# Query scores of the expert router issued one unit later in PSUM banks of their own, and two small reads of the attention at highest priority

## The chip, the cores and the metric

The kernel runs on one core of one Trainium2 chip. The metric is the device time of one execution in microseconds, shown as the median of the runs. The core has a matrix engine (TensorE, PE in the profile, with its weight loads on a row of their own, PEld), a vector engine (VectorE, DVE), an activation engine (ScalarE, ACT), GpSimd (POOL) and a queue for transfers (SyncE, SP). Each engine takes its own instructions strictly in the order in which they stand in its queue. TensorE writes to PSUM, eight banks of 128 partitions by 512 words of fp32.

## The reference

Two transformer blocks over 512 tokens of width 1024, batch 1. The first has a mixer of retention and sparse attention and a convolutional feed-forward part. The second has a mixer and then PEER, a layer that picks 16 of 16384 experts for each of 8 heads. The two places that the change touches are these, cut to what matters:

```
# first block, sparse attention, for a block of 128 queries
p_cmp = masked_softmax(q @ kc^T, valid_c)        # 31 compressed keys
p_slc = masked_softmax(q @ ks^T, mask)           # selected keys
p_win = masked_softmax(q @ kw^T, mask)           # window
...
# second block, PEER router
q = (x @ w_query).reshape(T, 8, 2, 128)
s = einsum('thpk,hpnk->thpn', q, sub_keys)       # 16 score groups of 128 keys
top_s, top_i = top_k(s, 16)
cand = top_s[:, :, 0, :, None] + top_s[:, :, 1, None, :]
best_s, best_pos = top_k(cand, 16)
gate = softmax(best_s)
```

## The kernel before

All matrix products with large weights are made of three passes: a weight tile of 128 by 1024 words (a unit) is loaded into `raw` (L192), ScalarE rounds it to `whi` (L200), VectorE or GpSimd takes the rest `wlo = raw - whi` (L201), and TensorE multiplies low by high, high by low and high by high (L206 to L208). `raw` has three buffers, `whi` and `wlo` eight each, so units are split up to eight ahead of their use. `proj_t` is one unit against all its tokens: 24 matmuls.

The instructions are written as a program in Python, and a planner then makes the order of each engine's queue: it simulates the engines and gives each free engine the ready instruction that stands earliest in the program. So an instruction can overtake earlier ones that are not ready in the simulated time. `high_priority` puts the instructions under it ahead of all others that are ready. What the planner believed of the durations fixes the order; the chip then follows that order with its own durations.

**Attention** (`attend`, tiles `tt` = 3, 2, 1, 0 of 128 queries). For a tile, four matmuls give the compressed scores (L599) into a bank of the group `as_` (banks 0, 1, 3 in turn). VectorE adds the mask bias in two instructions (L601). Then for each of two key groups, two branches and four heads: scores of 128 by 512 (L633, L635) into the next bank of the same group, the negated row maximum on VectorE (L637, `nm`), the exponential on ScalarE (L639), transposes (L647) and the product with the values (L654). The third head's scores of the first tile take bank 0 again, which the compressed scores held. The last tiles of retention (`retain`) stand just before: their normalisation is on VectorE (L575 to L584), with a power on GpSimd in the middle (L579).

**Router** (`route`). Sixteen units of the query weights: a projection of 24 matmuls into a bank of group `t` (banks 6, 7 in turn), a copy to `q` by ScalarE (L1100), four score matmuls (8 records of L1103) into the other bank of `t`, a copy to `sc` (L1105), and for each of four token tiles a top 16 on VectorE, five operations in `top16` (L1174 to L1178). After the sixteen units come the candidate sums, second top 16 and index arithmetic of four token tiles, nearly all on VectorE (L1111 to L1155); each `si` (L1141) is transposed by TensorE (L1166). Then `gates_dense` builds the dense gates from one-hot tiles (matmuls L1216, on tiles made by VectorE, ScalarE and GpSimd), spills them to memory, and `experts_out` reads them back and runs the output side of the experts.

`peer` puts 64 units of the experts' input side (`expert_in`, 24 matmuls of 384 columns, activation L1062) between the steps of `route` and `gates_dense`. The list `pace` says how many in how many steps: 3 in the first step, 2 in the next 15, 45 in the 32 after, 14 in the 24 steps of `gates_dense`. These last 14 use tiles of a pool that is opened when `route` has ended.

Of the kernel before, what the change touches and what calls it, by code (L numbers as in the profile page):

```python
# [2 lines left out]

# [4 lines left out]
F32 = mybir.dt.float32  # L8
# [4 lines left out]
AF = mybir.ActivationFunctionType  # L13
ALU = mybir.AluOpType
AX = mybir.AxisListType
# [3 lines left out]
S = 512  # L19
D = 1024  # L20
NT = 4
# [150 lines left out]
class Block:  # L172
# [413 lines left out]
    def attend(self, T, psp):  # L586
        tc, nc, a = self.tc, self.nc, self.a
# [3 lines left out]
        for tt in range(NT - 1, -1, -1):  # L591
            tok = slice(128 * tt, 128 * tt + 128)
            nk = 128 * (tt + 1)
            sums = T.tile([128, 3, 8], F32, name="sums")

            s = T.tile([128, 8, 32], F32, name="cs")
            ps = psp.tile([128, 4, 2, 32], F32, name="as_")
            for i in range(4):
                nc.tensor.matmul(ps[:, i], self.nqT[:, i, tok], self.kcT, start=True, stop=True)  # L599
            for g in range(2):  # L600
                nc.vector.tensor_tensor(s[:, 4 * g:4 * g + 4, :], ps[:, :, g, :],  # L601
                                        self.cst["cbias"][:, None, 32 * tt:32 * tt + 32].to_broadcast([128, 4, 32]),
                                        op=ALU.add)
            m = T.tile([128, 8], F32, name="cm")
            nc.vector.tensor_reduce(m, s, AX.X, ALU.max)
            nc.vector.tensor_tensor(s, s, m[:, :, None].to_broadcast([128, 8, 32]), op=ALU.subtract)
# [2 lines left out]
                                    op=ALU.mult)  # L609
# [15 lines left out]
            for g in range(2):  # L625
                pos = psp.tile([128, 2, 4, 64], F32, name="ao")
                for br in range(2):
                    po = pos[:, br]
                    for i in range(4):
                        h = 4 * g + i  # L630
                        ps = psp.tile([128, 512], F32, name="as_")
                        for part in range(2):
                            nc.tensor.matmul(ps[:, :nk], self.hl[:, h, tok], self.hh[:, 4 * part + 2 * g + br, :nk],  # L633
                                             start=part == 0, stop=False)
                        nc.tensor.matmul(ps[:, nk - 128:nk], self.identb, self.maskb, start=False, stop=True)  # L635
                        nm = T.tile([128, 1], F32, name="nm", bufs=4)
                        nc.vector.tensor_reduce(nm, ps[:, :nk], AX.X, ALU.max, negate=True)  # L637
                        p = T.tile([128, 512], F32, name="p", bufs=4)
                        e = nc.scalar.activation(p[:, :nk], ps[:, :nk], AF.Exp, bias=nm,  # L639
                                                 accum_out=sums[:, 1 + br, h:h + 1])  # L640
                        if tt == NT - 1 and g == 1:
                            k = 4 * br + i
                            with tc.issue_after(e.ins):
                                wout.append(self.unit(a["w_out"][k], eng=nc.gpsimd if i in WP else None))
                        pt = psp.tile([128, 4, 128], F32, name="at")
                        for b in range(tt + 1):
                            nc.tensor.transpose(pt[:, b, :], p[:, 128 * b:128 * b + 128], self.ident)  # L647
                        pT = T.tile([128, 4, 128], F32, name="pT", bufs=3)
                        if h % 2:
                            nc.vector.tensor_copy(pT[:, :tt + 1], pt[:, :tt + 1])  # L650
                        else:
                            nc.scalar.activation(pT[:, :tt + 1], pt[:, :tt + 1], AF.Copy)
                        for b in range(tt + 1):
                            nc.tensor.matmul(po[:, i, :], pT[:, b, :], self.vv[:, b, 128 * br + 64 * g:128 * br + 64 * g + 64],  # L654
                                             start=b == 0, stop=b == tt)
                    hs = slice(4 * g, 4 * g + 4)
                    sm = sums[:, 1 + br, hs]
                    nc.vector.tensor_scalar(sm, sm, 1e-30, None, op0=ALU.max)
                    nc.vector.reciprocal(sm, sm)
                    nc.vector.tensor_tensor(sm, sm, gt[:, 1 + br, hs], op=ALU.mult)  # L660
                    t = T.tile([128, 4, 64], F32, name="yt")
                    nc.vector.tensor_tensor(t, po, sm[:, :, None].to_broadcast([128, 4, 64]),
                                            op=ALU.mult)
                    nc.gpsimd.tensor_tensor(y[:, hs], y[:, hs], t, op=ALU.add)
                if tt and g == 0:
                    self.queries(T, tt - 1)
# [355 lines left out]
    def peer(self):  # L1022
        tc, nc, a = self.tc, self.nc, self.a
        dt = slice(128, S)
        n = S - 128
        with ExitStack() as c0:
            dr = c0.enter_context(tc.tile_pool(name="pdr", bufs=1, space=DRAM))
            self.actD = dr.tile([NSPILL, 128, n], F32, name="actD")
            self.gD = dr.tile([12, 128, 4096], F32, name="gD")
            P = c0.enter_context(tc.tile_pool(name="pe", bufs=1, reuse_waits="tile"))  # L1030
            self.acc0 = P.tile([128, D], F32, name="acc0")
            self.eid = P.tile([128, 128], I32, name="eid")
            self.gate0 = P.tile([128, 128], F32, name="gate0")
            with ExitStack() as c1:
                Q = c1.enter_context(tc.tile_pool(name="pra", bufs=1, reuse_waits="tile"))
                psp = _Banks(self.psum, t=[6, 7], u=[4, 5, 0], g=[1, 2, 3])
                sel = [Q.tile([128, NT - 1, 128], F32, name=f"sel{i}") for i in range(3)]
                iota = self.const(Q, "iota")
                pace = [(1, 3), (15, 2), (32, 45), (24, 14)]
                self.pend = []  # L1040
                work = [self.route(Q, psp, sel, iota), self.gates_dense(psp, sel, iota)]
                j, self.gpool = 0, None
                for n_, (steps, us) in enumerate(pace):
                    for i in range(steps):
                        _advance(work)
                        for _ in range((i + 1) * us // steps - i * us // steps):
                            act = self.expert_in(self.gpool or Q, psp, 2 * j, nc.vector if n_ == 2 else nc.gpsimd,
                                                 "ga" if self.gpool else "act")
                            nc.sync.dma_start(self.actD[j], act)
                            j += 1  # L1050
                assert j == NSPILL
                while work:
                    _advance(work)
            self.experts_out()
# [33 lines left out]
    def route(self, Q, psp, sel, iota):  # L1088
        tc, nc, a = self.tc, self.nc, self.a
        with tc.tile_pool(name="rt", bufs=1, reuse_waits="tile") as R:  # L1090
            sk = R.tile([128, 16, 128], F32, name="sk")
            nc.sync.dma_start(sk, a["skT"].rearrange("p (m n) -> p m n", m=16))
            val = R.tile([128, NT, 16, 16], F32, name="val")
            idx = R.tile([128, NT, 16, 16], U32, name="idx")
            for m in range(16):
                w = self.unit(a["w_q"][m])
                ps = psp.tile([128, S], F32, name="t")
                self.proj_t(ps, w, self.hh, self.hl)
                q = R.tile([128, S], F32, name="q", bufs=2)
                nc.scalar.activation(q, ps, AF.Copy)  # L1100
                ps = psp.tile([128, NT, 128], F32, name="t")
                for t in range(NT):
                    nc.tensor.matmul(ps[:, t, :], q[:, 128 * t:128 * t + 128], sk[:, m, :], start=True, stop=True)  # L1103
                sc = R.tile([128, NT, 128], F32, name="sc", bufs=2)
                nc.scalar.activation(sc, ps, AF.Copy)  # L1105
                for t in range(NT):
                    self.top16(R, sc[:, t, :], val[:, t, m, :], idx[:, t, m, :])
                yield
            for t in range(NT):
                cand = R.tile([128, 8, 16, 16], F32, name="cand")  # L1110
# [17 lines left out]
                for i in range(2):  # L1128
                    eq = R.tile([128, 8, 16, 16], F32, name="eq")
                    for h in range(0, 8, 4):  # L1130
# [4 lines left out]
                                                op=ALU.is_equal)  # L1135
                    nc.vector.tensor_tensor(eq, eq, fi[:, i::2, None, :].to_broadcast([128, 8, 16, 16]),
                                            op=ALU.mult)
# [6 lines left out]
                g = Q.tile([128, 8, 16], F32, name="g", bufs=2)  # L1144
# [160 lines left out]
def _advance(work, n=1):  # L1305
    while n and work:
        try:
            next(work[0])
            n -= 1
        except StopIteration:  # L1310
            work.pop(0)
# [54 lines left out]
```

## Time and profile before

| | us |
|---|---|
| median of three runs | 2283.4 |
| lowest, highest | 2283.37, 2287.0 |
| profiled execution, its time | 2284.21 |
| its span, first to last instruction | 2282.4 |
| TensorE busy in the span | 2201.8 (96%) |
| VectorE busy | 1680.1 (74%) |
| ScalarE busy | 922.4 (40%) |
| GpSimd busy | 690.0 (30%) |
| mean granted TensorE clock | 0.986 |

Busy time of a matmul is from its start to its modelled end, and consecutive ones overlap; the spacing of their starts says how fast they follow each other. The time of an execution is 1.8 us more than its span.

### The profile page before, as it was taken

Reading aid. Unit: us, or ns where it says so; the run is one execution under the profiler, and the core shown is the slowest. Engines: PE = TensorE matmul, PEld = TensorE weight load, DVE = VectorE, ACT = ScalarE, POOL = GpSimd, SP = SyncE. Lnnn points to the kernel's source line nnn. Section 1 sums busy time; section 2 is a strip of 40 time slices with the busy share of each in tenths; the row PEclk is TensorE's granted clock in tenths of the full one; section 3 lists DMA queues with packets and bytes.
Section 4 is the critical chain, followed back from the end, with each engine's and each line's share of the span. In section 5 each row is a group of like instructions: output and inputs, shape, how many; then the busy total and the mean of one; then the engine's idle time right before and its main releaser. Section 6 shows DMA issues by size and latency. Waiting matters only on the chain. (4 is left out here: it accounts for less than half of the span.)

```text
span 2282.4 us, 32112 instructions
## 1 busy us (share of the span) xinstructions
PE 2201.8 (96%) x11849; PEld 1952.1 (86%) x11849; DVE 1680.1 (74%) x3126; ACT 922.4 (40%) x1540; POOL 690.0 (30%) x558
## 2 busy tenths in 40 slices
PE   7998999999999999989999989889999999999997
PEld 6786878888889888877999989878888888888886
DVE  5347557888426478567799999678888787888888
ACT  4225444333325443342344468533333333333332
POOL 2223110000002223210000587533444444444445
PEclk9998999999999999999999999989999999999999
DMA  8324006767322221042355546799999999999996
GB/s 274 99 69 120 10 1 210 246 210 230 102 92 87 92 84 56 10 159 85 128 171 180 161 174 252 290 325 349 338 340 343 355 333 339 330 345 335 346 340 216
DMA packets 165645, 469.53 MB, mean 206 GB/s; under 512 B 18800, under 2 KB 62704, under 8 KB 165360
## 3 DMA queue, kind: packets, MB, share of 16 engines
q1 hardware_dynamic: 128624, 333.25, 42.7%
q0 software_dynamic: 36864, 134.23, 16.0%
q8 instruction: 93, 1.52, 0.3%
q14 instruction: 64, 0.52, 0.1%
HBM read 422.31 MB, written 39.85 MB: 202 GB/s over the span
## 5 line engine op out<-in xcount | busy, mean ns | idle before, releaser
L206 PE MATMUL b<-hh,wlo 128*128 128x384 f32 (+2 forms) x1872 | 655.5, 351 | 6.3 <-DVE wlo L201 3.1
L207 PE MATMUL b<-hl,whi 128*128 128x384 f32 (+2 forms) x1872 | 652.9, 349 | 3.3 <-DVE hl L288 3.2
L208 PE MATMUL b<-hh,whi 128*128 128x384 f32 (+2 forms) x1872 | 652.3, 349 | 0.0
L201 DVE TENSOR_TENSOR wlo<-raw,whi 128x1024 fp32r<-128x1024 f32 x375 | 455.3, 1222 | 201.4 <-ACT whi L200 195.4
L200 ACT ACTIVATE whi<-raw 128x1024 fp32r<-128x1024 f32 (+1 forms) x405 | 425.3, 1054 | 363.2 <-PE b L208 148.9
L206 PEld LDWEIGHTS b<-hh,wlo 128*128 128x128 f32 x1872 | 353.4, 189 | 34.2 <-DVE wlo L201 3.7
L207 PEld LDWEIGHTS b<-hl,whi 128*128 128x128 f32 x1872 | 354.2, 189 | 30.4 <-DVE hl L288 3.8
L208 PEld LDWEIGHTS b<-hh,whi 128*128 128x128 f32 x1872 | 353.9, 189 | 24.7
L206 PE MATMUL b<-whi,wl 128*128 128x512 f32 x768 | 299.9, 390 | 12.3 <-DVE wl L1262 12.3
L208 PE MATMUL b<-whi,wh 128*128 128x512 f32 x768 | 300.9, 392 | 0.0
L207 PE MATMUL b<-wlo,wh 128*128 128x512 f32 x768 | 300.8, 392 | 0.0
L201 POOL TENSOR_TENSOR wlo<-raw,whi 128x1024 fp32r<-128x1024 f32 x30 | 80.0, 2678 | 640.7 <-ACT whi L200 635.7
L1074 POOL DMA_INDIRECT grow<-in_p_ur_dram,eid x128 | 177.2, 1385 | 234.7 <-DVE gact L1077 166.9
L1074 POOL DMA_INDIRECT grow<-in_p_v_dram,eid x128 | 172.1, 1345 | 217.8 <-DVE acc L1079 132.8
L1062 ACT ACTIVATE act<-b 128x384 f32<-128x384 f32 x114 | 55.7, 492 | 382.4 <-PE b L208 301.4
L206 PE MATMUL b<-whi,hl 128*128 128x512 f32 (+1 forms) x464 | 178.9, 387 | 3.3 <-DVE hl L254 2.3
L206 PEld LDWEIGHTS b<-whi,wl 128*128 128x128 f32 x768 | 144.9, 189 | 41.4 <-DVE wl L1262 12.6
L208 PE MATMUL b<-whi,hh 128*128 128x512 f32 (+1 forms) x464 | 177.9, 384 | 0.0
L207 PE MATMUL b<-wlo,hh 128*128 128x512 f32 (+1 forms) x464 | 177.7, 383 | 0.0
L208 PEld LDWEIGHTS b<-whi,wh 128*128 128x128 f32 x768 | 144.7, 188 | 30.4
L207 PEld LDWEIGHTS b<-wlo,wh 128*128 128x128 f32 x768 | 144.8, 189 | 29.0
L1079 DVE SCALAR_TENSOR_TENSOR acc<-grow,gact,acc 128x1024 f32<-128x1024 f32 x127 | 162.7, 1281 | 3.4 <-DMA grow<-in_p_v_dram,eid 2.4
(296 smaller groups left out, 2953.6 us busy)
## 6 DMA issues: line engine op xcount, KB each, us to landing
raw<-in_p_u_dram SPq DMA_DIRECT2D x128, 512.0 KB
raw<-in_p_v_dram SPq DMA_DIRECT2D x128, 512.0 KB
raw<-in_w_adaT_dram SPq DMA_DIRECT2D x48, 512.0 KB
gD<-gst SPq DMA_DIRECT2D x48, 512.0 KB
gt<-gD SPq DMA_DIRECT2D x16, 1536.0 KB
raw<-in_w_up_dram SPq DMA_DIRECT2D x44, 512.0 KB
raw<-in_w_t_dram SPq DMA_DIRECT2D x32, 512.0 KB
acts<-actD SPq DMA_DIRECT2D x64, 192.0 KB
```

Of the source, the lines that this page charges most:

```text
L200: nc.scalar.activation(hi, raw, AF.Copy)
L201: (eng or nc.vector).tensor_tensor(lo, raw, hi.bitcast(F32), op=ALU.subtract)
L206: mm(out, al, bh, start=start, stop=False)
L207: mm(out, ah, bl, start=False, stop=False)
L208: mm(out, ah, bh, start=False, stop=stop)
L1062: self.nc.scalar.activation(act, ps, AF.Gelu)
L1074: nc.gpsimd.indirect_dma_start(out=g, out_offset=None, in_=rows[n], in_offset=bass.IndirectOffsetOnAxis(ap=self.eid[:, s:s + 1], axis=0))
L1079: nc.vector.scalar_tensor_tensor(self.acc0, g, act[:, s:s + 1], self.acc0, op0=ALU.mult, op1=ALU.add)
```

## The change

In `attend`, for the first tile (`tt` = 3) alone, the two bias additions of the compressed scores and the first four row maxima are put under `high_priority`. In `route`, the loop has 17 steps in place of 16: step m projects unit m and then issues the scores and the top 16 of unit m - 1; the scores are in banks of group `g` (1, 2, 3), which `gates_dense` uses later, and no longer in those of `t`. `pace` has 16 steps in place of 15 for the two experts' units, since `route` now has one step more.

```
+            with tc.high_priority() if tt == NT - 1 else nullcontext():
+                for g in range(2):
+                    nc.vector.tensor_tensor(s[...], ps[:, :, g, :], cbias, op=ALU.add)
...
-                        nc.vector.tensor_reduce(nm, ps[:, :nk], AX.X, ALU.max, negate=True)
+                        with tc.high_priority() if tt == NT - 1 and g + br == 0 else nullcontext():
+                            nc.vector.tensor_reduce(nm, ps[:, :nk], AX.X, ALU.max, negate=True)
...
-                pace = [(1, 3), (15, 2), (32, 45), (24, 14)]
+                pace = [(1, 3), (16, 2), (32, 45), (24, 14)]
...
-            for m in range(16):
-                w = self.unit(a["w_q"][m])
-                ps = psp.tile([128, S], F32, name="t")
-                self.proj_t(ps, w, self.hh, self.hl)
-                q = R.tile([128, S], F32, name="q", bufs=2)
-                nc.scalar.activation(q, ps, AF.Copy)
-                ps = psp.tile([128, NT, 128], F32, name="t")
-                for t in range(NT):
-                    nc.tensor.matmul(ps[:, t, :], q[:, 128 * t:128 * t + 128], sk[:, m, :], start=True, stop=True)
-                sc = R.tile([128, NT, 128], F32, name="sc", bufs=2)
-                nc.scalar.activation(sc, ps, AF.Copy)
-                for t in range(NT):
-                    self.top16(R, sc[:, t, :], val[:, t, m, :], idx[:, t, m, :])
+            qs = {}
+            for m in range(17):
+                if m < 16:
+                    w = self.unit(a["w_q"][m])
+                    ps = psp.tile([128, S], F32, name="t")
+                    self.proj_t(ps, w, self.hh, self.hl)
+                    qs[m] = R.tile([128, S], F32, name="q", bufs=2)
+                    nc.scalar.activation(qs[m], ps, AF.Copy)
+                if m:
+                    q = qs.pop(m - 1)
+                    ps = psp.tile([128, NT, 128], F32, name="g")
+                    for t in range(NT):
+                        nc.tensor.matmul(ps[:, t, :], q[:, 128 * t:128 * t + 128], sk[:, m - 1, :], start=True, stop=True)
+                    sc = R.tile([128, NT, 128], F32, name="sc", bufs=2)
+                    nc.scalar.activation(sc, ps, AF.Copy)
+                    for t in range(NT):
+                        self.top16(R, sc[:, t, :], val[:, t, m - 1, :], idx[:, t, m - 1, :])
                 yield
```

## Rows read from the trace of the kernel before

**Rows 1.** The page, busy time of each engine.
```profile
PE 2201.8 (96%) x11849; PEld 1952.1 (86%) x11849; DVE 1680.1 (74%) x3126; ACT 922.4 (40%) x1540; POOL 690.0 (30%) x558
```
**Rows 2.** Windows: stretch, length, busy PE, PEld, DVE, ACT, POOL, PE clock, DMA share, GB/s.
```profile
1062.00:1137.00 75.00, 74.74 (x400) 67.93 (x401) 49.55 (x238) 24.75 (x36) 2.40 (x1) 1.00 0.33 107
1137.00:1313.00 176.00, 176.00 (x1017) 175.43 (x1015) 173.65 (x388) 75.22 (x110) 30.81 (x10) 1.00 0.52 171
1313.00:1322.00 9.00, 0.82 (x3) 0.52 (x3) 8.93 (x13) 2.33 (x4) 5.86 (x5) 0.62 0.21 67
1322.00:1462.00 140.00, 139.44 (x1069) 138.69 (x1069) 135.51 (x359) 107.49 (x232) 119.75 (x99) 0.99 0.61 234
1491.00:2260.00 769.00, 769.00 (x3704) 677.65 (x3705) 627.18 (x814) 270.17 (x373) 343.39 (x251) 1.00 0.93 337
```
**Rows 3.** Waits of PE, 994 to 1330 us: total us, times, longest.
```profile
PE b L1166 <- DVE si L1141: 6.1, 1, 6.1
PE b L1103 <- ACT q L1100: 5.7, 8, 0.7
```
**Rows 4.** Timeline of PE, score matmuls: start, us, what, idle before.
```profile
1025.44 1.16 PE L1103 MATMUL b<-sk,q 128*128 128x128 f32 x8 [0.58 <-ACT q L1100]
...
1054.90 1.16 PE L1103 MATMUL b<-sk,q 128*128 128x128 f32 x8 [0.75 <-ACT q L1100]
...
1072.72 1.05 PE L1103 MATMUL b<-sk,q 128*128 128x128 f32 x8
...
1135.04 1.05 PE L1103 MATMUL b<-sk,q 128*128 128x128 f32 x8
```
**Rows 5.** Timeline of ACT, activations of successive experts' units.
```profile
1149.88 0.49 ACT L1062 ACTIVATE act<-b 128x384 f32<-128x384 f32 x1 [2.72 <-issue]
...
1166.52 0.49 ACT L1062 ACTIVATE act<-b 128x384 f32<-128x384 f32 x1 [2.72 <-issue]
```
**Rows 6.** Timeline of DVE, first and last work for one unit.
```profile
1041.10 1.23 DVE L201 TENSOR_TENSOR wlo<-raw,whi 128x1024 fp32r<-128x1024 f32 x1 [1.45 <-ACT whi L200]
1042.25 0.87 DVE L1174 MAX8 val<-sc 128x8 f32<-128x128 f32 x4
...
1046.73 0.28 DVE L1178 FIND_INDEX8 idx<-val,rest 128x8 uint32<-128x128 f32 x1
```
**Rows 7.** Timeline of DVE, end of the router: one shape, twice.
```profile
1298.05 2.35 DVE L1134 TENSOR_TENSOR eq<-abf,c_iota 128x1024 f32<-128x1024 f32 x2
...
1307.36 6.82 DVE L1134 TENSOR_TENSOR eq<-abf,c_iota 128x1024 f32<-128x1024 f32 x2
```
**Rows 8.** Timeline of PE, end of the router and first gates.
```profile
1319.11 0.45 PE L1166 MATMUL b<-c_ident,si 128*128 128x128 f32 x1 [6.07 <-DVE si L1141]
1321.66 4.52 PE L1216 MATMUL b<-gb,ga 128*128 128x128 f32 x22 [2.11 <-DVE gb L1213]
...
1335.01 5.89 PE L1216 MATMUL b<-gb,ga 128*128 128x128 f32 x48
```
**Rows 9.** Timeline of PE, scores of the first attention tile.
```profile
188.29 1.19 PE L633 MATMUL b<-hh,hl 128*128 128x512 f32 x2 [4.99 <-DVE cs L601]
...
198.56 0.71 PE L633 MATMUL b<-hh,hl 128*128 128x512 f32 x2
```
**Rows 10.** Timeline of DVE at the same place.
```profile
185.53 1.36 DVE L582 TENSOR_SCALAR rraw<-b,bmv,gr 128x128 f32<-128x128 f32 x4 [1.55 <-POOL gr L579]
...
187.66 0.49 DVE L601 TENSOR_TENSOR cs<-b,c_cbias 128x128 f32<-128x128 f32 x2
188.06 1.28 DVE L637 TENSOR_REDUCE nm<-b 128x1 f32<-128x512 f32 x2
```
**Rows 11.** Timeline of ACT at the same place.
```profile
188.81 1.28 ACT L639 ACT_TABLE_LOAD   x1 [12.38 <-issue]
190.11 0.69 ACT L639 ACTIVATE p<-b,nm 128x512 f32<-128x512 f32 x1
```
**Rows 12.** Windows after the wait; columns as in rows 2.
```profile
188.30:196.00 7.70, 6.38 (x21) 4.08 (x22) 6.53 (x13) 5.28 (x12) 1.28 (x1) 0.52 0.19 43
```

More of the change, by code (lines that the diff above doesn't have):

```diff
@@ L1 @@
 import numpy as np
-from contextlib import ExitStack
+from contextlib import ExitStack, nullcontext
 import concourse.bass as bass
@@ L599, in attend @@
                 nc.tensor.matmul(ps[:, i], self.nqT[:, i, tok], self.kcT, start=True, stop=True)
[L600 to L603, printed above, removed]
+            with tc.high_priority() if tt == NT - 1 else nullcontext():
+                for g in range(2):
+                    nc.vector.tensor_tensor(s[:, 4 * g:4 * g + 4, :], ps[:, :, g, :],
+                                            self.cst["cbias"][:, None, 32 * tt:32 * tt + 32].to_broadcast([128, 4, 32]),
+                                            op=ALU.add)
             m = T.tile([128, 8], F32, name="cm")
```

## The prediction

> **What bounds the kernel now.** I read the page first: TensorE is busy 96% of the span and no other engine comes near [rows 1]. An average hides where the other 4% lie, so next come the windows, cut where the work changes. From 1491 to 2260 us TensorE has no gap, with the transfers at 0.93 of their engines; nothing in the change touches that stretch. In the router, TensorE is busy throughout from 1137 to 1313, and VectorE nearly so (173.65 of 176). Then TensorE stands still for most of nine microseconds while VectorE works on (0.82 against 8.93 of 9.00), and from 1322 to 1462 both are full again [rows 2]. So VectorE is late once, at 1313, and TensorE sets the pace around it. The view of waits names the places: eight waits of the score matmuls for `q`, and one long wait for the last `si` of the router [rows 3]. A second one of that size stands in the attention, 4.99 us before the third head's scores [rows 9]. These three places are what the change can reach.
>
> **The router's scores.** The change takes the wait for `q` from between projection and scores; the instructions are the same. The waits shown add to 5.7 us [rows 3], but the start-to-start spacing is the better measure, since a busy time includes the pipeline's end. Where the scores directly follow their projection, a unit takes (1054.90 - 1025.44) / 4 = 7.365 us; five starts are in that run. Where the planner has put one experts' unit in between, it takes (1135.04 - 1072.72) / 6 = 10.387 us [rows 4]. An experts' unit alone takes (1166.52 - 1149.88) / 4 = 4.16 us [rows 5]. So a unit without a gap costs 10.387 - 4.16 = 6.23 us, and the gap costs 7.365 - 6.23 = 1.14 us. Eight gaps [rows 3] are 9.1 us. The other eight units are already covered by experts' units and gain nothing. After the change the next projection is the cover; it needs a free bank of `t` and a `w` tile, and both are there, as `t` now serves projections alone and units are split eight ahead. For the last unit, the second experts' unit of the new `pace` entry can fill the gap. If that cover were missing, one gap of 1.14 us would stay.
>
> Is VectorE fast enough? Its work for one unit runs from 1041.10 to 1047.01, 5.91 us [rows 6], against 6.23 us of TensorE. It just fits, so the scores stage stays TensorE's.
>
> **The wait at 1313.** The saving above starts VectorE's long tail sooner, and by more than 9.1 us. Before, eight experts' units ran among the scores; their only reason was the gap. Without gaps I expect the two that the program puts there. The last scores, which end at 1136.1 [rows 4], then end 9.1 + 6 x 4.16 = 34 us earlier, at 1102. VectorE's router ended at 1319.1 [rows 8], 183 us after the last scores. It also gets the splits of six more experts' units behind them, at 1.15 us each (1042.25 - 1041.10 [rows 6]), 7 us. It would end at 1102 + 183 + 7 = 1292. TensorE, with the same total of experts' units to do, runs out of them 9.1 us sooner than at 1313, at 1304. So VectorE would be done 12 us before it is needed, and the waits of 6.07 and 2.11 us go [rows 8]: 8.2 us. Behind them the clock stood lower (0.62 in the window [rows 2]); the first 22 gate matmuls took 4.52 / 22 = 0.205 us each and a later run of 48 took 5.89 / 48 = 0.123 [rows 8]. That is 0.082 x 22 = 1.8 us more. The bounds of this part are 0 (VectorE late as before) and 10.0; I take 10.0 because of the 12 us in hand.
>
> One rule speaks against those 12 us. In the router's end one pair of `eq` instructions took 2.35 us and the next such pair 6.82 [rows 7], while GpSimd was splitting weights (30.81 us busy in ten instructions, 1137 to 1313 [rows 2]). The Trainium skill, "SBUF — State Buffer", section "Who interferes with whom", says that VectorE instructions with two SBUF inputs and GpSimd instructions that read SBUF contend for a shared port pair, and one fully blocks the other. The row agrees. By the rule and by the row the same follows: VectorE's tail moves against GpSimd's splits and its 183 us may become longer by as much as another pair's 6.82 - 2.35 = 4.5 us, or by several such pairs; three use up the 12 us. This is the first rival below.
>
> **The attention.** VectorE's queue before the change had the bias additions behind the normalisation of the last retention tile. That waited 1.55 us for GpSimd, and the additions only ran at 187.66 [rows 10]; the third head's scores, which need bank 0 back, waited 4.99 us until 188.29 [rows 9]. The first row maximum stood behind as well and ended near 188.7 (188.06 + 1.28 / 2 [rows 10]), then came ScalarE's table load of 1.28 us and the first exponential, ending at 190.8 [rows 11]. After the change both additions and the first two maxima come before that normalisation. The wait of TensorE began at 188.29 - 4.99 = 183.3; a maximum of 0.64 us right there, the table load and an exponential of 0.69 end at 185.9. The chain is 4.9 us earlier. What is behind the moved ones, about 2.9 us of normalisation (1.36 and the batch of small ones), is of a tile whose result is read three tiles later, and its bank is not the scores' one, so nothing waits. TensorE's clock is 0.52 from 188.3 to 196 [rows 12], where two score matmuls take 1.19 us as against 0.71 later [rows 9]. A stall of some 2 us instead of 5 may leave the clock up: four pairs at 0.48 us are 1.9 us. Bounds: 0, as VectorE has 6.53 of 7.7 us of work there [rows 12] and could take over as the limit, and 4.9 + 1.9 = 6.8. I take 5.5, nearer the wait that the rows show. Nothing later takes it back, as the feed-forward part is TensorE's.
>
> **Sum.** 9.1 + 8.2 + 1.8 + 5.5 = 24.6 us. From the profiled execution's 2284.2 that is 2259.6; the median lies 0.8 lower. I forecast 2259.5.
>
> **The rivals.** (a) *VectorE stays late at the router's end*, because its tail grows or because the planner places the transposes too early for the chip's VectorE. For it: VectorE has hardly a free microsecond from 1137 on. Against: 12 us in hand. Then the 8.2 + 1.8 stay: 2284.2 - 14.6 = 2269.6. (b) *The attention gains nothing*, VectorE being the limit there; 2284.2 - 19.1 = 2265.1. (c) *The scores don't move*. The planner, not the program, makes the order, and half of the gaps were already filled by it; it could put the scores back where they were, if it finds them ready. Against: ready scores now stand behind a projection in the program. Only the attention is left: 2278.7. (d) *Slower.* TensorE takes its queue in order. If the planner believes VectorE done by 1292 and puts the last transposes there, but the chip's VectorE still ends near 1319, TensorE waits at that transpose with its experts' units queued behind it. The wait would be up to 1319 - 1292 = 27 us, in place of 8.2. It decides the sign above 24.6 us, three times the lateness seen; with 27 us and 2 us of low clock the time is 2284.2 - 24.6 + 29 = 2288.6.
>
> **How the numbers follow.** Likeliest, all three gains: 0.49. (a) 0.19, (b) 0.13, (c) 0.12, (d) 0.07. This kernel's measurement tells about 0.2%, 4.6 us. (c) lies at 0.24% under the profiled execution and 0.2% under the median, so I give two thirds of it to no change. Faster 0.49 + 0.19 + 0.13 + 0.04 = 0.85, no change 0.08, slower 0.07. The range takes in (a) and (b), with the attention at its low bound too in (a), 2284.2 - 9.1 = 2275.1; it leaves out (c) and (d). Below the forecast, the attention's upper bound gives 2258.3; if the chip's own waits around the first gates shrink as well (2 to 5 us more), 2253. Range 2253 to 2276.
>
> **What would show each step.** Score matmuls spaced 6.2 us without a wait for `q`, about two experts' units among them, last scores near 1102 less the attention's gain: the first step. No wait for `si` on TensorE at the start of the gates, and no dip of the clock there: the second. The third head's scores with no wait for `cs`, first exponential near 186, clock near 1 until 196: the third. The prediction is wrong if the score matmuls still wait, if experts' units still lie among the scores in number, or if TensorE stands before a transpose of `si` as long as before.

## The result and the profile after

The changed kernel takes 2265.83 us (median of six runs, 2264.93 to 2266.89), the kernel before 2283.39 in the runs beside it (2280.64 to 2287.0). The ratio is 0.9921, with a 95% interval of 0.9908 to 0.9934: 17.6 us faster, where 24 were forecast. The profiled execution has a span of 2264.4 us against 2282.4, 18.0 less.

The page of the changed kernel, busy time of each engine, answers to [rows 1]: TensorE does the same 11849 instructions in 9.7 us less busy time.

```profile
PE 2192.1 (97%) x11849; PEld 1947.6 (86%) x11849; DVE 1682.0 (74%) x3126; ACT 920.3 (41%) x1540; POOL 687.0 (30%) x558
```

Windows of the changed kernel, columns as in [rows 2]: the start of the attention, a later part of it, the scores, VectorE's tail, the first gates, the other gates, and the experts' stream.

```profile
188.30:196.00 7.70, 4.22 (x17) 2.68 (x18) 6.29 (x13) 4.75 (x12) 0.73 (x1) 0.62 0.20 46
206.00:222.00 16.00, 15.63 (x124) 13.93 (x123) 12.54 (x19) 13.01 (x25) 13.66 (x8) 1.00 0.39 133
1005.00:1098.00 93.00, 93.00 (x483) 80.45 (x482) 81.99 (x457) 30.01 (x45) 2.39 (x1) 1.00 0.27 91
1098.00:1282.00 184.00, 184.00 (x1064) 183.83 (x1064) 180.54 (x413) 78.23 (x114) 15.82 (x6) 1.00 0.52 172
1282.00:1310.00 28.00, 26.91 (x188) 26.49 (x187) 28.00 (x54) 17.56 (x36) 27.17 (x20) 1.00 0.52 175
1310.00:1437.00 127.00, 127.00 (x982) 127.00 (x980) 120.91 (x317) 98.56 (x209) 107.21 (x88) 1.00 0.65 243
1463.00:2240.00 777.00, 777.00 (x3740) 684.31 (x3741) 634.52 (x825) 270.51 (x376) 346.64 (x251) 1.00 0.93 336
```

The hole of [rows 2] at 1313 is gone: TensorE has no more than 1.1 us of idle time from the scores to the last gates, and the clock stays at 1.00. Its waits from 994 to 1330 us, against the list that [rows 3] is cut from, are one line:

```profile
PE b L1222 <- DVE gb L1219: 1.1, 2, 0.8
```

The timeline of its score matmuls (L1109 is L1103 of before), beside [rows 4], and below them the last transpose of an `si`:

```profile
1005.99 1.05 PE L1109 MATMUL b<-sk,q 128*128 128x128 f32 x8
1012.34 1.05 PE L1109 MATMUL b<-sk,q 128*128 128x128 f32 x8
...
1092.71 1.05 PE L1109 MATMUL b<-sk,q 128*128 128x128 f32 x8
1096.75 1.05 PE L1109 MATMUL b<-sk,q 128*128 128x128 f32 x8
...
1308.01 0.27 PE L1172 MATMUL b<-c_ident,si 128*128 128x128 f32 x1
```

Starts are 6.35 us apart, with no wait. In the rows left out one start is farther behind (1044.07 to 1054.63, with an experts' unit in between), and a second experts' unit covers the last `q`, between 1092.71 and 1096.75: two units, as forecast. VectorE was done with that `si` at 1284.0, 24 us before its transpose.

The rest of the change came out otherwise. Two groups of the changed kernel's instructions by tile (min/median/max ns, first and last start) give the end of the matmul stream and of VectorE's accumulation of gathered rows for token tile 0, which is made beside it:

```profile
L206 PE MATMUL b<-whi,wl x768: 387/389/795, 1463.0 to 2240.3; 128*128 128x512 f32 x192
L1081 DVE SCALAR_TENSOR_TENSOR acc<-grow,gact,acc x127: 1275/1280/1324, 1517.1 to 2245.8; 128x1024 f32<-128x1024 f32 x127
```

The same two of the kernel before:

```profile
L206 PE MATMUL b<-whi,wl x768: 387/389/794, 1490.7 to 2268.5; 128*128 128x512 f32 x192
L1079 DVE SCALAR_TENSOR_TENSOR acc<-grow,gact,acc x127: 1275/1280/1322, 1537.4 to 2263.7; 128x1024 f32<-128x1024 f32 x127
```

The matmul stream ends 28.2 us sooner, more than the sum that was forecast. The accumulation ends only 17.9 us sooner, and now it is the later of the two. GpSimd's timeline of the changed kernel shows it waiting for that accumulation to close the output:

```profile
2236.88 0.94 POOL L1076 DMA_INDIRECT grow<-in_p_v_dram,eid  x1 [0.30 <-issue]
2247.27 2.48 POOL L1282 TENSOR_TENSOR acc<-acc,g 128x512 f32<-128x512 f32 x2 [9.46 <-DVE acc L1081]
```

### The profile page after: what moved, and what is told of

Read it like the earlier page. It is cut to its first block, busy times and chain, and to the rows that moved or that the text cites. A ratio compares the mean times of both kernels' runs of the same rounds, so it can differ in the third digit from the quotient of the medians.

```text
span 2264.4 us, 32116 instructions
## 1 busy us (share of the span) xinstructions
PE 2192.1 (97%) x11849; PEld 1947.6 (86%) x11849; DVE 1682.0 (74%) x3126; ACT 920.3 (41%) x1540; POOL 687.0 (30%) x558
## 4 chain that ended last, share of the span: by engine, by line
PE 84%; DVE 6%; issue 3%; DMA 2%; POOL 2%; ACT 1%; SPq 0%; DVEq 0%; POOLq 0%; ACTq 0%
PE b L206 25%; PE b L207 25%; PE b L208 25%; PE b L1222 4%; PE b L656 1%; POOL grow L1076 1%; PE b L1109 1%; DMA grow<-in_p_v_dram,eid 1%; DMA gD<-gst 1%; PE b L649 1%; PE b L516 0%; PE b L634 0%; PE b L251 0%; PE b L944 0%; DMA K<-kcm 0%
```

## The experiments

**Which half does it.** `route_only` has the changed router and no priorities; `attn_only` has the priorities and the router of before.

```
# route_only, on the changed kernel, at both places
-  with tc.high_priority() if tt == NT - 1 ... else nullcontext():
+  with nullcontext():
# attn_only: before's route() and pace, the changed attend()
```

> The changed kernel without the two high priorities: the router's part alone. Theory (the two parts add, and at the end the gathers of token tile 0 set the time): TensorE's last matmuls come 23 us earlier than before, the end only 13 to 18 us earlier: 2265 to 2270. Rival (the attention's 5 us are luck of the order and come or go with any edit): an attention as before in this run and an end 18 us earlier all the same, about 2266. Second rival (the parts don't add, the router's part alone gives less than 9 us): above 2274.

> The kernel before with the two high priorities alone, the router as before. Theory: the attention ends 5 us earlier as in the changed kernel, though its first row maximum and first exponential stay at 188 and 190 us; matmuls and gathers both move by 5 us: 2278.4. Rival (the gathers hold the end, so nothing is seen): 2283. Rival (what I predicted, the first exponential near 186): the same time, but another trace.

`route_only` took 2267.67 us (2267.02 to 2274.08; ratio 0.9941, 0.9919 to 0.9964), `attn_only` 2279.6 (0.9982, 0.9972 to 0.9991). The router is nearly all of it. The priorities are worth 1.8 us between `route_only` and the changed kernel by their medians (by the two ratios 4.6, but their intervals overlap), and 2.8 to 4.1 in `attn_only` by its median and its ratio.

**Lag or banks.** `lag_same_banks` issues the scores one unit later but leaves them in the banks of `t`; `banks_no_lag` gives them the banks of `g` but issues them right after their projection, as before (with the 15 steps of before in `pace`). Both have the two priorities.

```
# lag_same_banks
-  ps = psp.tile([128, NT, 128], F32, name="g")
+  ps = psp.tile([128, NT, 128], F32, name="t")
# banks_no_lag: the loop of before, and in it
-  ps = psp.tile([128, NT, 128], F32, name="t")     # the scores'
+  ps = psp.tile([128, NT, 128], F32, name="g")
```

> The changed kernel with the late scores put into the banks of the projections again. Theory (the lag does it; a projection then waits only for the copy of the unit before, which the scores in between hide to within some 0.3 us): score matmuls without a wait of 0.7 us, spacing 6.3 to 6.7 us, end as in the changed kernel, 2264 to 2270. Rival (the own banks are what helps): waits of about 1 us per unit or experts' units in between as before, last scores after 1115, end above 2272.

> The kernel before with the two high priorities and the scores in the banks of the gates, but issued directly after their projection. Theory (the lag does it): waits for q and spacing of 7.4 us as before, eight experts' units among the scores, 2278 to 2281, as with the high priorities alone. Rival (the banks do it): spacing near 6.3 us, under 2270.

`lag_same_banks` took 2268.44 us (0.9927, 0.991 to 0.9943), `banks_no_lag` 2266.23 (0.9913, 0.9897 to 0.993). I had taken the lag for the cause; `banks_no_lag` shows that it isn't needed. TensorE's timeline of the scores in `banks_no_lag`:

```profile
1019.96 1.05 PE L1105 MATMUL b<-sk,q 128*128 128x128 f32 x8
1026.31 1.05 PE L1105 MATMUL b<-sk,q 128*128 128x128 f32 x8
1032.66 1.05 PE L1105 MATMUL b<-sk,q 128*128 128x128 f32 x8
```

The spacing is again 6.35 us, without a wait for `q`, although the program asks for the scores first: the planner puts nearly all of the next projection ahead of them by itself, once it has a bank (the first scores come after 46 matmuls, 24 of the first projection and 22 of the second). Before, `t` went round two banks, so every projection took one of them and every score group the other. The next projection had to wait until `q` had been copied out of its bank, and so it couldn't cover that same copy. The lag alone also takes the waits for `q` away, but the last scores stand at 1117.1 us in place of 1097.9, as more experts' work is placed among them: from 1054.82 on its scores are 9.52 us apart. Behind them TensorE waits 2.1 us for `si` and 4.3 for `gb`, and its first product of the experts' stream comes at 1474.0, 11 us after the changed kernel's. So the near tie in time isn't a near tie of the two routers: the gathers of `lag_same_banks` kept the early start that those of the changed kernel lost (the table further down).

**Does VectorE's early end pay?** `more_experts` puts ten experts' units in place of two among the scores and eight fewer behind them.

```
-  pace = [(1, 3), (16, 2), (32, 45), (24, 14)]
+  pace = [(1, 3), (16, 10), (32, 37), (24, 14)]
```

> The changed kernel with the pace of the router set so that ten experts' units in place of two stand among the sixteen projections and score groups, and eight fewer behind them. Theory (step two of the prediction: VectorE's router tail starts with the last scores and TensorE's units run out behind it, so eight units of 4.16 us among the scores put the last score near 1131, the last index near 1314, and TensorE out of work near 1305): TensorE waits 5 to 10 us for `si` again, the first expert product on TensorE comes 5 to 9 us after 1463.0, the matmul stream ends at 2245 to 2250, and the time is 2267 to 2275. Rival (the planner fills the hole with other work, or VectorE isn't what TensorE waits for there): no wait for `si` over 2 us, the first expert product within 2 us of 1463.0, and the time within 3 us of 2266.

It took 2279.93 us (2278.07 to 2281.74; 0.9978, 0.9968 to 0.9988), 14 more than the changed kernel and 5 over the top of what was expected. The last scores are at 1128.1 and the last `si` at 1307.0. TensorE's timeline shows the wait of [rows 8] again, with the clock lower behind it (0.74 from 1310 to 1320):

```profile
1300.32 0.34 PE L208 MATMUL b<-hh,whi 128*128 128x384 f32 x1
1309.40 0.45 PE L1172 MATMUL b<-c_ident,si 128*128 128x128 f32 x1 [8.74 <-DVE si L1147]
1310.22 0.47 PE L1172 MATMUL b<-c_ident,g 128*128 128x128 f32 x1 [0.37 <-ACT sel L1173]
1312.23 7.04 PE L1222 MATMUL b<-gb,ga 128*128 128x128 f32 x48 [1.54 <-DVE gb L1219]
```

With 1.24 us for the `si` before, these waits are 11.9 us, and the first product of the experts' stream comes 12.1 us later (1475.1 for 1463.0). The wait came as forecast; its price was set too low, probably because I had counted the one wait alone.

**What sets the end.** Sixteen of the 256 gathers and their products are left out, in the changed kernel and in the kernel before.

```
+  if h == 7 and n == "p_ur":
+      if s == 112:
+          nc.vector.memset(act[:, hs], 0.0)
+      yield
+      continue
```

> The changed kernel with 16 of the 256 gathers left out (those of the last head's first table, with their products, so part of the computation of token tile 0 is missing). Theory: the chain of gathers ends some 16 x 3.05 = 49 us earlier, so that the matmuls set the end again; the end follows the last matmul by 14 us as before: 2240 + 14 + 2 = 2256. Rival (the last 10 us are the finishing work, not the gathers): no gain, 2265 or at most 1 to 2 us less.

> The kernel before with the same 16 of 256 gathers left out. Theory: there the chain of gathers and the matmuls ended nearly together, the end was 13.9 us after the last matmul as against 9.2 us in the changed kernel without the 16: a gain of about 5 us, 2277 to 2279. Rival (the matmuls alone set the end there): 2282. Rival (the gathers set it alone by more): under 2272.

`after_no16` took 2250.62 us (0.985, 0.9827 to 0.9872), 15 less than the changed kernel. The accumulation ends at 2209.9 there, the matmul stream at 2240.6, where it was; the span ends 9 us behind that. `before_no16` took 2278.96 (0.9971, 0.996 to 0.9982), some 4 to 7 less than before (2283.4; 0.0029 of it is 6.6). So the chain of gathers set the end in both, by some 5 us before and by 15 after.

**Can the chain be made shorter?** Four attempts, each on the changed kernel. `first4` issues four gathers ahead of the experts' stream in the program in place of one; `products_hp` gives VectorE's products of gathered rows the highest priority; `grows5` and `rows5_act3` have five row buffers, with the room taken from one or the other kind of activation buffer.

```
# first4
-  _advance(gather)
+  _advance(gather, 4)
# products_hp, around the three products in gather()
+  with tc.high_priority():
# grows5, rows5_act3
-GROWS = 4
+GROWS = 5
# grows5: acts bufs=3 to 2;  rows5_act3: act bufs=4 to 3
```

> The changed kernel with the first four gathers and their products issued before the experts' output side instead of one. Theory: the gathers' chain lost its start because its first product stood on VectorE behind the gates' product, which waited for a transfer until 1458.6; with four products ahead of it the chain starts up to 14 us earlier and the end gains up to 10 us: 2256 to 2260. Rival (the chain catches up or loses later anyway, its start doesn't matter): 2265.

> The changed kernel with VectorE's products and accumulations of the gathered rows issued at the highest priority; four row buffers as they are. Theory (each turn of a row buffer is some 10 us from issue to use and 1.5 us from use to the next issue, and a part of the 10 us is a row that lies landed while VectorE does other work): the products come nearer to the landing, the last accumulation comes 9 us or more before 2245.8, and the time is 2252 to 2260. Rival 1 (the 10 us are nearly all the gather itself): the last accumulation stays within 4 us of 2245.8 and the time within 3 us of 2266. Rival 2 (VectorE's queue is in order, so a product placed early stands and waits for its row, and the `wl` behind it come late): TensorE's waits for `wl` grow over 15 us and the time is over 2268.

> The changed kernel with five buffers for gathered rows in place of four (and two for reloaded activations in place of three, to make room). Theory (a gather's round trip of about 12 us over its buffers paces the chain, and the chain ends last): the chain gets ahead of the matmuls and the end follows the last matmul by some 9 us, as in the run with 16 gathers less: 2250 to 2254. Rival (the transfer engines, 0.93 busy, set the round trip, so a fifth buffer only lengthens it): 2262 to 2266.

> The changed kernel with five buffers for the rows that the gathers fetch in place of four, and the room taken from the experts' activations `act` (three buffers in place of four); `acts` keeps its three. Theory (in the changed kernel the chain of 256 gathers of token tile 0 sets the end, 9 us behind what the matmul stream would allow): the last accumulation comes well before 2209.9, the place it has with sixteen gathers fewer, the matmul stream ends near 2240 as before it, and the time is 2250 to 2257. Rival 1 (activation buffers were what made the other kernel with five rows slow, and three `act` are too few too): TensorE waits for `wl` by more than the 7 us of now, and the time is over 2266. Rival 2 (a fifth row starts more traffic that slows the weights' transfers): the gathers end early, no wait for `wl` behind `act`, but TensorE waits for weights (`whi`, `wlo`) and the time is over 2266.

`first4` took 2267.78 us (0.9929, 0.9906 to 0.9952) and `products_hp` 2265.97 (0.9916, 0.9894 to 0.9939). Neither says anything on the chain: the planner left the first gathered products behind the same wait for `gt`, at 1459.9 and 1460.2 us in place of 1460.0.

`grows5` took 2312.99 us (1.0121, 1.0104 to 1.0138) and `rows5_act3` 2311.31 (1.0118, 1.0095 to 1.0141), both slower than the kernel before. The gathers did get faster: in `rows5_act3` the last accumulation stands at 2161.2 in place of 2245.8. But the matmul stream ended 59 us later, at 2299.0. TensorE's waits in `rows5_act3` from 1300 us on (7.0 us and one wait for `wl` in the changed kernel), and below, one window of it:

```profile
PE b L206 <- DVE wl L1268: 44.8, 13, 6.8
PE b L206 <- DVE wlo L201: 3.0, 2, 2.8
...
1500.00:2110.00 610.00, 579.64 (x2729) 505.38 (x2727) 508.33 (x659) 196.22 (x275) 304.41 (x224) 0.98 0.95 348
```

The same window of the changed kernel:

```profile
1500.00:2110.00 610.00, 610.00 (x2955) 538.67 (x2954) 494.89 (x643) 217.01 (x301) 270.86 (x194) 1.00 0.94 339
```

`grows5`, where the other buffers are cut, waits for `wl` 44.5 us, 13 times; so what the two have in common counts, the fifth row. In the 610 us the queues issue 224 gathers in place of 194 and 133 weight units in place of 145, each of 512 KB, while all transfers together rise only from 339 to 348 GB/s. That fits a chain that takes its rows out of the same transfers as the weights, but it isn't shown: TensorE waits for `wl` and hardly for weights (`wlo`, 3.0 us), once every 55 us or so, right behind the experts' unit that this `wl` is made from. The order of the queues may be as much to blame; no run tells the two apart.

**Does the start of the chain decide?** The table is worked out from the first product of the experts' stream, the first gathered product and the last accumulation of each trace, in us after the first of these.

| kernel | first gathered product | last accumulation |
|---|---|---|
| before | -16.8 | 773.0 |
| `attn_only` | -17.6 | 773.4 |
| `lag_same_banks` | -15.2 | 773.6 |
| after | -3.0 | 782.8 |
| `route_only`, `banks_no_lag` | -3.0 | 783.2, 782.8 |
| `more_experts` | -2.9 | 782.6 |

There are two families, ten us apart, and the ten us are about what the changed kernel gave back. VectorE's timeline shows the difference. Before, one gathered product stands ahead of the wait for `gt`:

```profile
1473.85 1.22 DVE L1077 CUSTOM_DVE_ANT_0 grow<-grow,h 128x1024 f32<-128x1024 f32 x1
1475.00 0.08 DVE L1077 DVE_READ_ACCUMULATOR2_ANT gact<- 128x1 f32 x1
1485.01 1.96 DVE L1257 TENSOR_TENSOR act<-act,gt 128x384 f32<-128x384 f32 x4 [9.93 <-DMA gt<-gD]
```

After, all stand behind it, the rows being asked for since 1432.75:

```profile
1448.74 1.23 DVE L201 TENSOR_TENSOR wlo<-raw,whi 128x1024 fp32r<-128x1024 f32 x1 [0.68 <-ACT whi L200]
1458.61 1.50 DVE L1263 TENSOR_TENSOR act<-act,gt 128x384 f32<-128x384 f32 x3 [8.64 <-DMA gt<-gD]
1460.02 1.22 DVE L1079 CUSTOM_DVE_ANT_0 grow<-grow,h 128x1024 f32<-128x1024 f32 x1
```

`rows_first` forces four gathered products ahead of it by a data dependency.

```
-  _advance(gather)
+  _advance(gather, 4)
+  zero = P.tile([128, 1], F32, name="zero")
+  nc.vector.tensor_scalar(zero, self.gact[:, 3:4], 0.0, None, op0=ALU.mult)
...
-  nc.vector.tensor_tensor(act, act, gt, op=ALU.mult)
+  if j < 8:
+      nc.vector.scalar_tensor_tensor(act, act, zero, gt, op0=ALU.add, op1=ALU.mult)
```

> The changed kernel with VectorE's first four products of gathered rows put ahead of the first products of activations and `gt`: the latter take as an addend a zero made from the fourth gathered product, so they can't be placed before it; the values are the same. Measured so far, in all kernels: where one gathered product runs before VectorE waits for `gt`, the last accumulation ends 773 us after the first product of the experts' matmuls (773.0, 773.4, 773.6 in three kernels); where it stands behind that wait, 783 us after it (782.8, 783.2, 782.6, 782.8 in four). Theory (the ten us of the gain that are given back are this order of VectorE's queue: the rows lie landed while VectorE waits for `gt`, and the chain of gathers starts late by that): the four products run before 1458, the first product of the experts' matmuls stays within 3 us of 1463.0, the last accumulation comes 8 to 14 us before 2245.8 and the time is 2251 to 2259. Rival 1 (the chain of gathers ends where the traffic of gathers and weights together lets it, whatever its start): the four products come early, the last accumulation stays within 4 us of 2245.8 and the time within 3 us of 2266. Rival 2 (the rows land only when `gt` does, so the products of activations and the matmuls now wait for them): the first product of the experts' matmuls comes more than 3 us later than 1463.0, and the time is 2262 to 2272.

It took 2267.54 us (0.9923, 0.991 to 0.9937): no gain. Yet the chain did what the theory says: products from 1449.5 on, the last accumulation at 2238.3, 7.5 us sooner, and 772.6 after the start of the stream (1465.7). What ate the gain is the matmul stream, which ends at 2255.4. It starts 2.7 us later, behind a wait for `wl` of 10.0 us (7.0 in the changed kernel), and lasts 789.7 us in place of 777.3, at clock 1.00 and without a further wait. TensorE's timeline of the changed kernel, then of `rows_first`:

```profile
1700.16 0.39 PE L206 MATMUL b<-whi,wl 128*128 128x512 f32 x1
...
1703.56 0.39 PE L206 MATMUL b<-whi,wl 128*128 128x512 f32 x1
```

```profile
1702.61 0.39 PE L206 MATMUL b<-whi,wl 128*128 128x512 f32 x1
...
1708.91 0.40 PE L206 MATMUL b<-whi,wl 128*128 128x512 f32 x1
```

Fifteen starts in 3.40 us are 0.227 us each, 27 in 6.30 are 0.233. Over 2304 such matmuls 0.006 us make 14 us, about the 12.4 that the stream grew by. In the program's allocation the small tile `zero` moves all tiles behind it: the stationary operands `wh` and `wl` begin at byte 214048 and 220192 of a partition, 32 past a multiple of 64, in place of 214016 and 220160, multiples of 64; the weights didn't move. The mean spacing is 0.228 in all thirteen other kernels. The experts' input matmuls of the same stretch (128x384), whose operands all stayed where they were, are 0.173 us apart (median) in `rows_first` as in the changed kernel. That the place is the cause fits all of this but wasn't tried by itself, and neither was `rows_first` with a `zero` of 64 bytes. So whether an earlier start of the chain pays in time is open: here it was hidden by the slower stream.

## Why the prediction was right, and where it was not

The side and the range held; the likeliest time was 6 us too low. Two terms of different sign were not in the sum at all (5.3 and -10.2 us, last point), so that it came this near is partly luck.

- *The scores* (9.1 us). Right in size: (7.365 - 6.345) x 8 = 8.2 us, since a unit without a gap takes 6.345 us and not 6.23. The last copy to `sc` is at 1097.9, where 1102 less the attention's gain was forecast. The reason was only half seen. The prediction named the bank of `t` as a thing that the next projection needs and has after the change; that the shared ring of `t` had made the gap in the order of before, and that the lag wasn't needed, `banks_no_lag` showed.
- *The wait at 1313* (8.2 + 1.8 us). Right. VectorE is done 24 us before TensorE comes to the last transpose, twice the 12 forecast; no wait, no lower clock. Its tail hardly grew: 183.8 us from the last copy of `sc` to the last `si`, 180.5 before. The contention that the prediction feared (the Trainium skill, "SBUF — State Buffer", section "Who interferes with whom") took less than feared: the last pairs of `eq` took 2.90 and 4.57 us, where [rows 7] has 2.35 and 6.82, with GpSimd busy for 15.82 us in that stretch. By GpSimd's timelines the traces agree with that rule: beside the 2.35 it stood idle until 1300.51, and beside the 6.82 and the 4.57 it was splitting weights. `more_experts` brings both back by taking VectorE's lead away. Rival (a), VectorE late all the same, fell. So did (c), as the scores moved, and (d).
- *The attention* (5.5 us). The mechanism was wrong. The timeline of VectorE in the changed kernel still has the retention's normalisation (L582) ahead of the additions and the first maximum, and ScalarE's first exponential starts at 190.11, where it did [rows 10, 11]. VectorE's rows, then ScalarE's and TensorE's:

```profile
185.73 1.37 DVE L582 TENSOR_SCALAR rraw<-b,bmv,gr 128x128 f32<-128x128 f32 x4 [1.54 <-POOL gr L579]
187.13 0.69 DVE L584 TENSOR_TENSOR yr<-rraw,yr 128x512 f32<-128x512 f32 x1
187.86 0.29 DVE L602 TENSOR_TENSOR cs<-b,c_cbias 128x128 f32<-128x128 f32 x1
188.07 1.28 DVE L639 TENSOR_REDUCE nm<-b 128x1 f32<-128x512 f32 x2
```

```profile
190.11 0.69 ACT L641 ACTIVATE p<-b,nm 128x512 f32<-128x512 f32 x1
```

```profile
190.94 1.12 PE L649 MATMUL b<-c_ident,p 128*128 128x128 f32 x4 [7.44 <-ACT p L641]
```

The highest priority moves an instruction only ahead of others that are ready with it; the normalisation must have been placed earlier in the planner's time. TensorE's wait only changed its name: 7.4 us for `p` in place of the 4.99 of [rows 9] and 1.3. The last exponential still comes 5.1 us sooner (320.23 for 325.30), and the traces show where. Near 215 us TensorE waits 1.9 us for `yt` without the priorities and 0.4 with them. In its timeline, of before, `route_only` and the changed kernel:

```profile
217.43 1.10 PE L654 MATMUL b<-vv,pT 128*128 128x64 f32 x8 [1.93 <-DVE yt L662]
```

```profile
216.85 1.10 PE L656 MATMUL b<-vv,pT 128*128 128x64 f32 x8 [1.90 <-DVE yt L664]
```

```profile
215.97 2.00 PE L656 MATMUL b<-vv,pT 128*128 128x64 f32 x16 [0.37 <-DVE yt L664]
```

Behind that wait the clock fell to 0.50, the lower of its two levels, from about 219 to 226 us in before and `before_no16`, but not in `route_only`, whose attention has the same code. One window, of before, `before_no16`, `route_only` and the changed kernel:

```profile
220.00:224.00 4.00, 4.00 (x21) 4.00 (x21) 2.44 (x8) 2.60 (x4) 3.62 (x3) 0.50 0.39 131
220.00:224.00 4.00, 4.00 (x21) 4.00 (x20) 3.15 (x8) 2.27 (x4) 3.78 (x3) 0.50 0.39 136
220.00:224.00 4.00, 4.00 (x37) 3.84 (x37) 4.00 (x8) 2.52 (x5) 3.62 (x2) 1.00 0.51 146
220.00:224.00 4.00, 4.00 (x28) 3.56 (x27) 3.93 (x4) 2.15 (x3) 4.00 (x3) 1.00 0.73 247
```

From the first exponential to the last, before and `before_no16` take 135.2 us, `route_only` 132.0, and all eleven kernels with the priorities 130.0 to 130.2, with the clock at 1.00 from 214 to 300 us in each. So the priorities give some 1.9 us, and 3.2 more against an execution whose clock fell there, which agrees with the 2 to 4 us by the times. A shorter wait that leaves the clock up is what the prediction hoped for, but at another place than it said. How the moved maxima shorten the wait for `yt` isn't settled.

- *"Nothing in the change touches that stretch"* [rows 2] and *"Nothing later takes it back"*. This is the step that failed. The matmul stream moved by 28.2 us, more than the 24.6, as 5.3 us of another wait went as well (TensorE waits for `wl` at its start 7.0 us, 12.3 before). But I read in the window only that TensorE has no gap, and took its stream for the end. The chain of gathers beside it had set the end by some 5 us already; the change put its first product behind the wait for `gt`, and 10 us went back: 28.2 - 10.2 = 18.0, the gain of the span. The 5.3 and the 10.2 may be two sides of one thing: that wait for `wl` is 6.6 to 8.1 us in the nine kernels whose first gathered product stands behind the wait for `gt`, and 9.0 to 13.0 in the five where it stands ahead. From the forecast's terms, by the traces: 24.6 - 0.9 (scores) - 0.4 (attention) + 5.3 (`wl`) - 10.2 (gathers) = 18.4. Rival (b) names 2265.1, all but the measured time, but by luck and not with its cause: the attention did come sooner, by 5.1 us in the trace, and without the gathers' 10.2 us the forecast would have been beaten.

## What to carry to other kernels

Where two things of one loop take turns in a ring of two banks, each gets always the same one, and in that order nothing can be moved ahead to cover the copy out of it: give each a ring of its own before reordering by hand. Before a gain is carried to the end of a kernel, look at what else ends there, within the size of the gain: here a chain on the queues of GpSimd and VectorE set the end by some 5 us while TensorE's stream filled the profile. Where the transfers are at 0.94, widening such a chain can cost more than it gives: a fifth row buffer ended the chain 85 us sooner and the kernel 45 us later. Starting it sooner ended it 7.5 us sooner; what that is worth in time no run has shown yet.

## What the runs showed of the hardware

The spacing of 128x512 matmuls was 0.227 us in the changed kernel and 0.233 in `rows_first`, at the same granted clock of 1.00; of their operands only the stationary ones lay elsewhere, 32 bytes on. So a tile of four bytes a partition, which takes 32 bytes here, came with 12 us on a stream of 777; one kernel only shows it.

Executions of one order differ in the attention. From 214 to 218 us TensorE was busy for 2.07 us in the trace of before, 2.09 in `before_no16` and 2.10 in `route_only`, whose attention is the same code; behind that the clock fell to 0.50 for some 7 us in the first two and stayed at 1.00 in the third, which was 3.2 us faster to the last exponential. With the priorities TensorE was busy for 3.63 of these 4 us in the changed kernel, and none of the eleven traces with them shows the fall.
